# A two-layer matmul with gelu: the opening takes half the rows of a and twice the columns of b, the other rows come later

## Chip, cores and metric

The kernel runs on one core of a Trainium2 chip. The metric is the device time of one execution in microseconds. Times in one set of rounds come from one chip; the sets fell on several chips, so each kernel is compared with the kernel before as it ran in the same rounds.

Terms: PE is the tensor engine (matmuls and transposes), DVE the vector engine (casts and copies), ACT the scalar engine (gelu, casts and copies), SP the queue that issues loads and stores. PSUM is the memory that PE writes. A float32 load is cast to bf16 before PE can use it, so "cast at" tells when a load was usable. A later load is one after the opening; k is the contraction index, cut in eight slices of 128.

## The reference, cut to what matters

```
a: 1024 x 1024, b: 1024 x 2048, c: 2048 x 1024, all float32
h = a @ b
h = 0.5 * h * (1 + tanh(sqrt(2/pi) * (h + 0.044715 * h**3)))
out = h @ c
```

## The kernel before

All matmuls run in bf16 with float32 sums. The first layer makes h transposed, tile by tile: a column tile t of b (128 columns) is the stationary operand, and half of a's rows, transposed, is the moving operand of 512 columns. That gives 16 tiles x 2 halves x 8 contraction slices = 256 matmuls. The second layer has another 256, counted as full width. a has to be transposed by PE first, which takes 64 transposes of 128 x 128.

The opening loads one contraction slice of all of a and of three column tiles of b per step, and fills six PSUM banks (three tiles, two halves):

```python
    for k in range(KT):
        ...                                     # k == 0 in three parts, one of them on the ACT queue
            nc.sync.dma_start(out=st, in_=av[:, :, ts(k, 128)])   # 512-byte runs
            nc.sync.dma_start(out=bt, in_=bv[:, k, 0:W0])         # W0 = 384: 1536-byte runs
    ...
    for _ in range(7):                          # warm-up
        nc.tensor.matmul(wps, warm[:, 0:128], warm, start=True, stop=True)
    ...
    for k in range(KT):
        ...                                     # casts of a and b
        for h in range(2):
            pt = tpool.tile([128, H], BF16, name="pt")
            for j in range(4):
                nc.tensor.transpose(pt[:, ts(j, 128)], ab[:, 4 * h + j, :], ident)
            ...                                 # copy to aT[k][h], DVE or ACT
        if k > 0:
            mm0(k - 1, 1)
        mm0(k, 0)
    mm0(KT - 1, 1)
```

After it come the other 13 column tiles of b, in loads of growing run length through four staging buffers, then c, and each tile is multiplied with both halves of a (`mm1`), followed by gelu on ACT. The second layer and the stores end the kernel.

## Time and profile before

| | before |
|---|---|
| time, median of 4 runs in the rounds with the change | 132.34 us (132.29 to 132.39) |
| span in the profile | 130.6 us |
| first matmul after the opening | 26.86 us |
| first matmul of the second layer | 71.93 us |
| last work of PE | 127.23 us |

From 26.86 us on PE never waits, so all that can be gained lies before, and whatever is added to PE's work later is lost one for one. The prediction below shows the lines.

### The profile page before, as it was taken

The page shows a single profiled execution, that of the slowest core. Times are in us where ns is not written, and L with a number is a line of the kernel's source. Part 1 is how long each engine was busy: PE and PEld are TensorE (multiplying, and loading weights), DVE is VectorE, ACT ScalarE, POOL GpSimd, SP SyncE. Part 2 cuts the span into 40 slices and gives each one's busy share as a digit, 9 for nine tenths or more (in the row PEclk, how much of TensorE's full clock was granted, in tenths as well). Part 3 has the DMA queues.
Part 4 walks back from the last instruction along what each step waited for, and adds up shares of the span by engine and source line. Part 5 has one row for each costly group of instructions (what it writes and reads, how often), then busy time and mean ns, then how long its engine had stood idle before and what let it go on. Part 6 is the DMA issues. An engine that isn't in the chain of part 4 may idle for free.

```text
span 130.6 us, 1457 instructions
## 1 busy us (share of the span) xinstructions
PE 120.7 (92%) x599; PEld 56.1 (43%) x599; DVE 39.0 (30%) x58; ACT 29.0 (22%) x50; POOL 0.7 (1%) x6
## 2 busy tenths in 40 slices
PE   6479998879999999999999999999999999999990
PEld 2144443334444444444444444444444444444580
DVE  0154544243543355345500022222222222211121
ACT  4135453863333333333333100000000000000000
POOL 2000000000000000000000000000000000000000
PEclk9977999999999999999999999999999999999999
DMA  2999999999999999999000022221111222222231
GB/s 40 287 308 310 307 310 309 295 303 359 393 385 398 408 410 405 412 409 360 25 0 0 5 80 80 80 80 72 58 55 64 79 80 80 80 80 80 80 123 40
DMA packets 20390, 25.25 MB, mean 193 GB/s; under 512 B 800, under 2 KB 14368, under 8 KB 20384
## 3 DMA queue, kind: packets, MB, share of 16 engines
q1 hardware_dynamic: 20240, 24.97, 56.7%
q10 hardware_dynamic: 144, 0.20, 1.0%
q8 instruction: 4, 0.07, 0.2%
q14 instruction: 2, 0.02, 0.1%
HBM read 20.97 MB, written 4.19 MB: 193 GB/s over the span
## 4 chain that ended last, share of the span: by engine, by line
PE 77%; DMA 16%; DVE 2%; SPq 1%; ACT 0%; issue 0%; DVEq 0%
PE ps L149 42%; PE ps L126 35%; DMA a_st<-in_a_dram 10%; DMA st<-in_b_dram 6%; SPq L65 1%; DVE ab L84 1%; PE pt L90 1%; DVE b_sb L108 1%; ACT aT L94 0%; SPq L62 0%; SPq L60 0%; DVE ot L141 0%; DVE ab L85 0%; DVEq L84 0%
## 5 line engine op out<-in xcount | busy, mean ns | idle before, releaser
L149 PE MATMUL ps<-c_sb,hT 128*128 128x512 bf16 (+1 forms) x272 | 55.5, 366 | 0.0
L126 PE MATMUL ps<-aT,b_sb 128*128 128x512 bf16 x208 | 45.1, 379 | 1.3 <-DVE b_sb L108 1.3
L149 PEld LDWEIGHTS <-hT 128*128 128x128 bf16 x272 | 26.6, 98 | 28.9
L126 PEld LDWEIGHTS <-b_sb 128*128 128x128 bf16 x208 | 20.3, 98 | 26.1 <-DVE b_sb L108 1.8
L141 DVE COPY ot<-ps 128x512 f32<-128x512 f32 (+1 forms) x17 | 11.2, 660 | 51.5 <-PE ps L149 51.5
L128 ACT ACTIVATE hT<-ps 128x512 bf16<-128x512 f32 x26 | 15.5, 597 | 29.4 <-PE ps L126 29.4
L114 DVE CAST c_sb<-st 128x2048 bf16<-128x2048 f32 x8 | 9.8, 1227 | 10.7 <-DMA st<-in_c_dram 10.7
L79 PE MATMUL ps<-aT,b_sb 128*128 128x512 bf16 x48 | 12.7, 402 | 0.0
L108 DVE CAST b_sb<-st 128x2048 bf16<-128x2048 f32 (+1 forms) x8 | 8.2, 1027 | 12.4 <-DMA st<-in_b_dram 12.4
L90 PE MATMUL pt<-ident,ab 128*128 128x128 bf16 x64 | 6.1, 232 | 4.0 <-DVE ab L84 3.5
L90 PEld LDWEIGHTS <-ab 128*128 128x128 bf16 x64 | 4.0, 102 | 8.9 <-DVE ab L84 7.4
L84 DVE CAST ab<-a_st 128x512 bf16<-128x512 f32 x8 | 3.4, 427 | 10.8 <-DMA a_st<-in_a_dram 10.8
L79 PEld LDWEIGHTS <-b_sb 128*128 128x128 bf16 x48 | 4.6, 103 | 4.4 <-issue 0.8
L86 ACT ACTIVATE b_sb<-b_st 128x384 bf16<-128x384 f32 x8 | 4.2, 523 | 8.2 <-DMA b_st<-in_b_dram 8.2
L94 ACT ACTIVATE aT<-pt 128x512 bf16<-128x512 bf16 x8 | 4.8, 597 | 4.5 <-PE pt L90 4.5
L73 PE MATMUL pt<-warm 128*128 128x512 bf16 x7 | 3.2, 630 | 1.2 <-DVE warm L45 1.2
L92 DVE COPY aT<-pt 128x512 bf16<-128x512 bf16 x8 | 3.4, 423 | 1.9 <-PE pt L90 1.9
L85 DVE CAST ab<-a_st 128x512 bf16<-128x512 f32 x8 | 3.4, 420 | 0.5 <-DMA a_st<-in_a_dram 0.5
L120 ACT ACTIVATE hT<-ps 128x512 bf16<-128x512 f32 x6 | 3.0, 615 | 0.3 <-PE ps L79 0.3
L73 PEld LDWEIGHTS <-warm 128*128 128x128 bf16 x7 | 0.9, 140 | 2.6 <-issue 1.4
L70 ACT ACT_TABLE_LOAD x1 | 1.3, 1283 | 1.2 <-PEq L166 1.2
L45 DVE MEMSET warm<- 128x256 uint32 x1 | 0.3, 272 | 0.9 <-PEq L166 0.9
(7 smaller groups left out, 1.1 us busy)
## 6 DMA issues: line engine op xcount, KB each, us to landing
st<-in_c_dram SPq DMA_DIRECT2D x8, 1024.0 KB, 9.1
st<-in_b_dram SPq DMA_DIRECT2D x5, 1024.0 KB, 9.4
out_dram<-ot SPq DMA_DIRECT2D x15, 256.0 KB, 2.0
a_st<-in_a_dram SPq DMA_DIRECT2D x7, 512.0 KB, 6.2
st<-in_b_dram SPq DMA_DIRECT2D x3, 512.0 KB, 8.6
b_st<-in_b_dram SPq DMA_DIRECT2D x7, 192.0 KB, 6.3
a_st<-in_a_dram SPq DMA_DIRECT2D x2, 256.0 KB, 5.2
out_dram<-ot SPq DMA_DIRECT2D x2, 128.0 KB, 1.9
```

The lines of the kernel that those rows point to most:

```text
L73: nc.tensor.matmul(wps, warm[:, 0:128], warm, start=True, stop=True)
L79: nc.tensor.matmul(ps[t][h], b_sb[:, k, ts(t, 128)], aT[k][h], start=(k == 0), stop=(k == KT - 1))
L84: nc.vector.tensor_copy(ab[:, 0:4, :], a_st[k][:, 0:4, :])
L86: nc.scalar.activation(b_sb[:, k, 0:W0], b_st[k], AF.Copy)
L90: nc.tensor.transpose(pt[:, ts(j, 128)], ab[:, 4 * h + j, :], ident)
L94: nc.scalar.activation(aT[k][h], pt, AF.Copy)
L108: nc.vector.tensor_copy(b_sb[:, kh:kh + kn, ds(t0 * 128, w)], sv)
L114: nc.vector.tensor_copy(c_sb[:, t0:t0 + 2, :], sv)
L126: nc.tensor.matmul(p, b_sb[:, k, ts(t, 128)], aT[k][h], start=(k == 0), stop=(k == KT - 1))
L128: nc.scalar.activation(hT[t][h], p, AF.Gelu_apprx_tanh)
L141: nc.vector.tensor_copy(ot, p)
L149: nc.tensor.matmul(p, hT[t][h][:, ts(j, 128)], c_sb[:, t, ds(q0, w)], start=(t == 0), stop=(t == NT - 1))
```

## The change

Its intent: let PE start the dense part sooner. The opening needs only half the rows of a (2 MB in place of 4), and takes six column tiles of b with them (3 MB in place of 1.5), so the same 48 matmuls stand on fewer bytes, in longer runs. Then come four more column tiles for this half, then the last six. The other rows of a are loaded after all of b, as whole rows (4096-byte runs), and are transposed ("turned") one block of 128 rows after each of the last four groups of the first half. Then the second half runs over all 16 tiles. Three smaller things change with it: slice 0 of b goes over the SP queue like all the rest (before, over ACT's), DVE makes all copies of transposes (before, ACT made half of them), and there are ten warm-up matmuls in place of seven.

```diff
-    N0 = 3
+    N0 = 6
+    N1 = 4
-            nc.sync.dma_start(out=st, in_=av[:, :, ts(k, 128)])
-            nc.sync.dma_start(out=bt, in_=bv[:, k, 0:W0])
+    for k, n in ((0, 1), (1, 1), (2, 2), (4, 2), (6, 2)):
+        load_a0(k, n)              # rows 0 to 511, n slices: runs of n x 512 bytes
+        for i in range(n):
+            load_b0(k + i)         # 768 columns: 3072-byte runs
-    for _ in range(7):
+    for _ in range(10):
...                                # opening: 4 transposes and 6 matmuls a slice
+    for k in range(0, KT, 2):      # second block: 4 tiles, contraction outside
+        load_b(k, 2, W0, W1)
+        ...
+    for n0 in range(W0 + W1, N, W2):        # third block: 6 tiles, W2 = 384
+        for k in range(0, KT, 4):
+            load_b(k, 4, n0, W2)
+    for j in range(4):                      # the other half of a
+        nc.sync.dma_start(out=st, in_=av[:, 4 + j, :])
+    def turn(j):
+        nc.vector.tensor_copy(ab, a1[j])
+        for k in range(KT):
+            nc.tensor.transpose(pt[:, k, :], ab[:, ts(k, 128)], ident)
+        nc.vector.tensor_copy(aT[1][:, :, ts(j, 128)], pt)
+    for t in range(N0 + N1, NT):
+        mm1(t, 0)
+        if t >= NT - 4:
+            turn(t - (NT - 4))
+    for t in range(NT):
+        mm1(t, 1)
```

More of the change, by code (lines that the diff above doesn't have):

```diff
@@ L25 @@
     H = 512
-    N0 = 3
+    N0 = 6
     W0 = N0 * 128
+    N1 = 4
+    W1 = N1 * 128
     av = a.rearrange("(mt p) k -> p mt k", p=128)
@@ L34 @@
     consts = ctx.enter_context(tc.tile_pool(name="consts", bufs=1))
+    keep = ctx.enter_context(tc.tile_pool(name="keep", bufs=1))
     astage = ctx.enter_context(tc.tile_pool(name="astage", bufs=4))
     abf = ctx.enter_context(tc.tile_pool(name="abf", bufs=3))
-    keep = ctx.enter_context(tc.tile_pool(name="keep", bufs=1))
-    b0stage = ctx.enter_context(tc.tile_pool(name="b0stage", bufs=4))
+    b0stage = ctx.enter_context(tc.tile_pool(name="b0stage", bufs=5))
     stage = ctx.enter_context(tc.tile_pool(name="stage", bufs=4))
@@ L47, with load_a0, load_b0 @@
     make_identity(nc, ident)
-    aT = [[keep.tile([128, H], BF16, name=f"aT{k}_{h}") for h in range(2)] for k in range(KT)]
+    aT = [keep.tile([128, KT, H], BF16, name=f"aT{h}") for h in range(2)]
     b_sb = keep.tile([128, KT, N], BF16, name="b_sb")
     c_sb = keep.tile([128, NT, P], BF16, name="c_sb")
-    hT = [[keep.tile([128, H], BF16, name=f"hT{t}_{h}") for h in range(2)] for t in range(NT)]
-    a_st, b_st = [], []
-    for k in range(KT):
-        st = astage.tile([128, MT, 128], F32, name="a_st")
-        bt = b0stage.tile([128, W0], F32, name="b0_st")
-        if k == 0:
-            nc.sync.dma_start(out=st[:, 0:4, :], in_=av[:, 0:4, ts(k, 128)])
-            nc.scalar.dma_start(out=bt, in_=bv[:, k, 0:W0])
-            nc.sync.dma_start(out=st[:, 4:8, :], in_=av[:, 4:8, ts(k, 128)])
-        else:
-            nc.sync.dma_start(out=st, in_=av[:, :, ts(k, 128)])
-            nc.sync.dma_start(out=bt, in_=bv[:, k, 0:W0])
-        a_st.append(st)
-        b_st.append(bt)
+    hT = [keep.tile([128, NT, H], BF16, name=f"hT{h}") for h in range(2)]
+    a_st, b_st = {}, {}
+    def load_a0(k, n):
+        st = astage.tile([128, 4, 256], F32, name="a_st")
+        nc.sync.dma_start(out=st[:, :, 0:n * 128], in_=av[:, 0:4, ds(k * 128, n * 128)])
+        for i in range(n):
+            a_st[k + i] = st[:, :, ts(i, 128)]
+    def load_b0(k):
+        st = b0stage.tile([128, W0], F32, name="b0_st")
+        nc.sync.dma_start(out=st, in_=bv[:, k, 0:W0])
+        b_st[k] = st
+    for k, n in ((0, 1), (1, 1), (2, 2), (4, 2), (6, 2)):
+        load_a0(k, n)
+        for i in range(n):
+            load_b0(k + i)
     g = consts.tile([128, 1], F32, name="g")
@@ L71, with mm0 @@
     wps = tpool.tile([128, H], F32, name="pt")
-    for _ in range(7):
+    for _ in range(10):
         nc.tensor.matmul(wps, warm[:, 0:128], warm, start=True, stop=True)
-    ps = [[ppool.tile([128, H], F32, name="ps") for _ in range(2)] for _ in range(N0)]
-    def mm0(k, h):
+    ps = [ppool.tile([128, H], F32, name="ps") for _ in range(N0)]
+    def mm0(k):
         for t in range(N0):
-            nc.tensor.matmul(ps[t][h], b_sb[:, k, ts(t, 128)], aT[k][h],
+            nc.tensor.matmul(ps[t], b_sb[:, k, ts(t, 128)], aT[0][:, k, :],
@@ L80, in mm0 @@
                              start=(k == 0), stop=(k == KT - 1))
     for k in range(KT):
-        ab = abf.tile([128, MT, 128], BF16, name="ab")
-        nc.vector.tensor_copy(ab[:, 0:4, :], a_st[k][:, 0:4, :])
-        nc.vector.tensor_copy(ab[:, 4:8, :], a_st[k][:, 4:8, :])
-        nc.scalar.activation(b_sb[:, k, 0:W0], b_st[k], AF.Copy)
-        for h in range(2):
-            pt = tpool.tile([128, H], BF16, name="pt")
-            for j in range(4):
-                nc.tensor.transpose(pt[:, ts(j, 128)], ab[:, 4 * h + j, :], ident)
-            if h == 0:
-                nc.vector.tensor_copy(aT[k][h], pt)
-            else:
-                nc.scalar.activation(aT[k][h], pt, AF.Copy)
@@ L95 @@
-        if k > 0:
-            mm0(k - 1, 1)
-        mm0(k, 0)
-    mm0(KT - 1, 1)
-    def load_b(t0, nt):
-        w = nt * 128
-        kn = 2048 // max(w, 256)
-        for kh in range(0, KT, kn):
-            st = stage.tile([128, 2048], F32, name="st")
-            sv = st[:, 0:kn * w].rearrange("p (k n) -> p k n", k=kn)
-            nc.sync.dma_start(out=sv, in_=bv[:, kh:kh + kn, ds(t0 * 128, w)])
-            nc.vector.tensor_copy(b_sb[:, kh:kh + kn, ds(t0 * 128, w)], sv)
+        ab = abf.tile([128, 4, 128], BF16, name="ab")
@@ new lines, with gelu @@
+        nc.vector.tensor_copy(ab, a_st[k])
+        pt = tpool.tile([128, H], BF16, name="pt")
+        for j in range(4):
+            nc.tensor.transpose(pt[:, ts(j, 128)], ab[:, j, :], ident)
+        nc.vector.tensor_copy(aT[0][:, k, :], pt)
+        for i in range(2):
+            nc.scalar.activation(b_sb[:, k, ts(i, W0 // 2)], b_st[k][:, ts(i, W0 // 2)], AF.Copy)
+        if k > 0:
+            mm0(k - 1)
+    mm0(KT - 1)
+    def gelu(t, h, p):
+        nc.scalar.activation(hT[h][:, t, :], p, AF.Gelu_apprx_tanh)
@@ new lines, with load_b @@
+    for t in range(N0):
+        gelu(t, 0, ps[t])
+    def load_b(k0, kn, n0, w):
+        st = stage.tile([128, 2048], F32, name="st")
+        sv = st[:, 0:kn * w].rearrange("p (k n) -> p k n", k=kn)
+        nc.sync.dma_start(out=sv, in_=bv[:, k0:k0 + kn, ds(n0, w)])
+        nc.vector.tensor_copy(b_sb[:, k0:k0 + kn, ds(n0, w)], sv)
+    ps = [(tpool if t < 2 else ppool).tile([128, H], F32, name="pt" if t < 2 else "ps")
+          for t in range(N1)]
+    for k in range(0, KT, 2):
+        load_b(k, 2, W0, W1)
+        for i in range(2):
+            for t in range(N1):
+                nc.tensor.matmul(ps[t], b_sb[:, k + i, ds(W0 + t * 128, 128)], aT[0][:, k + i, :],
+                                 start=(k + i == 0), stop=(k + i == KT - 1))
@@ L110, in load_c, with mm1 @@
+    for t in range(N1):
+        gelu(N0 + t, 0, ps[t])
+    def mm1(t, h):
+        p = ppool.tile([128, H], F32, name="ps")
+        for k in range(KT):
+            nc.tensor.matmul(p, b_sb[:, k, ts(t, 128)], aT[h][:, k, :],
+                             start=(k == 0), stop=(k == KT - 1))
+        gelu(t, h, p)
+    W2 = 384
+    for n0 in range(W0 + W1, N, W2):
+        for k in range(0, KT, 4):
+            load_b(k, 4, n0, W2)
     def load_c(t0):
@@ L114, in load_c @@
         nc.vector.tensor_copy(c_sb[:, t0:t0 + 2, :], sv)
-    load_b(3, 1)
-    load_b(4, 1)
-    for h in range(2):
-        for t in range(N0):
-            nc.scalar.activation(hT[t][h], ps[t][h], AF.Gelu_apprx_tanh)
-    def mm1(t):
-        for h in range(2):
-            p = ppool.tile([128, H], F32, name="ps")
-            for k in range(KT):
-                nc.tensor.matmul(p, b_sb[:, k, ts(t, 128)], aT[k][h],
-                                 start=(k == 0), stop=(k == KT - 1))
-            nc.scalar.activation(hT[t][h], p, AF.Gelu_apprx_tanh)
-    load_b(5, 1)
-    load_b(6, 2)
-    load_b(8, 4)
-    load_b(12, 4)
+    a1 = []
+    for j in range(4):
+        st = astage.tile([128, K], F32, name="a_st")
+        nc.sync.dma_start(out=st, in_=av[:, 4 + j, :])
+        a1.append(st)
+    def turn(j):
+        ab = abf.tile([128, K], BF16, name="ab1")
+        nc.vector.tensor_copy(ab, a1[j])
+        pt = tpool.tile([128, KT, 128], BF16, name="pt")
+        for k in range(KT):
+            nc.tensor.transpose(pt[:, k, :], ab[:, ts(k, 128)], ident)
[4 more added lines that the diff above has]
+            turn(t - (NT - 4))
     for t in range(0, NT, 2):
         load_c(t)
-    for t in range(N0, NT):
-        mm1(t)
+    for t in range(NT):
+        mm1(t, 1)
     def store(mt, q0, w, p):
-        ot = opool.tile([128, w], F32, name="ot", padded_shape=[128, H])
-        nc.vector.tensor_copy(ot, p)
-        nc.sync.dma_start(out=out[ts(mt, 128), ds(q0, w)], in_=ot)
+        ot = opool.tile([128, H], F32, name="ot")
+        nc.vector.tensor_copy(ot[:, 0:w], p)
+        nc.sync.dma_start(out=out[ts(mt, 128), ds(q0, w)], in_=ot[:, 0:w])
     for mt in range(MT):
@@ L148 @@
             for t in range(NT):
-                nc.tensor.matmul(p, hT[t][h][:, ts(j, 128)], c_sb[:, t, ds(q0, w)],
+                nc.tensor.matmul(p, hT[h][:, t, ts(j, 128)], c_sb[:, t, ds(q0, w)],
                                  start=(t == 0), stop=(t == NT - 1))
```

## The prediction

> **What bounds the kernel now.** I read the page's strip of slices first, then the chain that ended last, then the DVE timeline, because the casts there start when a load lands. The strip, from the page of the kernel before (busy tenths in 40 slices of 3.27 us; granted clock in tenths; GB/s of all loads and stores):
> ```profile
> PE   6479998879999999999999999999999999999990
> ...
> PEclk9977999999999999999999999999999999999999
> DMA  2999999999999999999000022221111222222231
> GB/s 40 287 308 310 307 310 309 295 303 359 393 385 398 408 410 405 412 409 360 25 0 0 5 80 80 80 80 72 58 55 64 79 80 80 80 80 80 80 123 40
> ```
> From slice 9 on PE is full. Only the first eight slices have holes, and there the DMA runs at about 309 GB/s, against 393 to 412 later: same engines, other run lengths. The chain (start, us, what):
> ```profile
> 9.12 6.23 DMA a_st<-in_a_dram
> ...
> 18.33 7.76 DMA st<-in_b_dram
> 26.09 0.02 issue
> 26.11 0.70 DVE b_sb L108
> 26.81 0.05 issue
> 26.86 45.07 PE ps L126 x208
> 71.93 55.31 PE ps L149 x272
> 127.23 0.02 issue
> 127.26 0.42 DVE ot L141
> ```
> Up to 26.86 loads set the pace; after that PE never waits. 45.07/208 is 216.7 ns a matmul, and the last one ends at 127.23; the remaining 3.37 us of the 130.6 us span (the last copy, the last store, the close) are not touched. So the change is worth what it moves the end of PE's work, and the timed 132.33 us moves with it. The DVE timeline, whole opening to first c load (start, length):
> ```profile
> 20.10 0.43 DVE L84 CAST ab<-a_st 128x512 bf16<-128x512 f32 x1 [0.98 <-DMA a_st<-in_a_dram]
> ...
> 22.43 0.43 DVE L84 CAST ab<-a_st 128x512 bf16<-128x512 f32 x1 [0.99 <-DMA a_st<-in_a_dram]
> ...
> 26.11 0.69 DVE L108 CAST b_sb<-st 128x1024 bf16<-128x1024 f32 x1 [2.33 <-DMA st<-in_b_dram]
> 27.74 0.69 DVE L108 CAST b_sb<-st 128x1024 bf16<-128x1024 f32 x1 [0.94 <-DMA st<-in_b_dram]
> 29.46 0.69 DVE L108 CAST b_sb<-st 128x1024 bf16<-128x1024 f32 x1 [1.03 <-DMA st<-in_b_dram]
> 32.35 1.23 DVE L108 CAST b_sb<-st 128x2048 bf16<-128x2048 f32 x1 [2.20 <-DMA st<-in_b_dram]
> 35.06 1.23 DVE L108 CAST b_sb<-st 128x2048 bf16<-128x2048 f32 x1 [1.48 <-DMA st<-in_b_dram]
> 37.78 1.23 DVE L108 CAST b_sb<-st 128x2048 bf16<-128x2048 f32 x1 [1.49 <-DMA st<-in_b_dram]
> ```
> One slice of k (512 KB of a in 512-byte runs, 192 KB of b in 1536-byte runs) lands every 2.33 us. PE needs less: eight transposes at about 0.07 and six matmuls at 0.217, 1.86 us.
>
> **What the skill says.** Four places bear on this.
> (1) The Trainium skill, "DMA: Bandwidth & Descriptors", section "Why small descriptors are slow (HBM only)": each packet carries a fixed overhead. The trace agrees. With 16 engines, 512 KB in 512-byte runs is 64 packets an engine in 1.69 us (27.74 less 26.11, and 29.46 less 27.74, averaged): 26.4 ns each. 1 MB in 4096-byte runs (c, casts at 45.76 and 48.31) is 16 packets in 2.56 us: 160 ns. The straight line is 7.3 ns plus 0.0373 ns a byte. It gives 83.7 ns at 2048 bytes; measured 2.70/32 = 84.4.
> (2) Same page, section "Why a DMA increments its semaphore by 16 and not by 1": a load counts as landed only when each of its engines is done, so a slow engine delays the landing though the mean rate holds. The trace suggests it: the first load after the opening was usable 3.17 us after the last opening b (ACT cast at 22.92), where its own bytes need 1.69; the rate stayed near 295 GB/s meanwhile.
> (3) The Trainium skill, "TensorE: Matmul & The Clock Gate", Part 1 (the HAM clock gate): a window of some 3.4 us with too little PE work halves the clock for the next. Here the windows view shows a granted clock of 0.50 from 8.0 to 11.0, with full clock on both sides: about 3.4 us.
> (4) The Trainium skill, "VectorE: DVE Perf Modes", section "Why PSUM operands drop a tier": bf16 out of PSUM goes at most two elements a cycle. The trace has 423 ns for 512 bf16 (L92) against 691 for 512 float32 (L141), which fits.
>
> **The change, part by part.**
> *Opening.* It takes 2 MB of a and 3 MB of b, 5 MB in place of 5.5 MB, and in longer runs. Packets per engine: two a slices alone, 32 of 512 bytes each, 0.845 us; three a pairs, 32 of 1024 bytes (45.5 ns), 1.456; eight b slices, 8 of 3072 bytes (121.9 ns), 0.975. Sum 1.69 + 4.37 + 7.80 = 13.86 us. The same line gives 2.21 for a slice of before, measured 2.33, so I add 5%: 14.55. Before, eight slices were 18.64 and the last b landed at 22.92, an offset of 4.28. After, the last b lands between 18.1 and 18.8; I take **18.5**, 4.4 us sooner.
> *PE in the opening.* Four transposes (0.29) and six matmuls (1.30) a slice, 1.59, against a supply of about 1.75: PE has nearly no slack to catch up. Transposes of slice 1 come before the matmuls of slice 0; a slice 1 lands near 7.2 (two a slices and one b, from data that begin to flow at 3.1, plus about 1.1 of landing), so matmuls start near 8.1. The three more warm-up matmuls bridge only to about 5.2. I expect the half clock from 7.9 to 11.3 again; it costs some 1.7 us, because here PE, not only DMA, is full. End of the opening on PE: 8.1 + 8 x 1.30 + 6 x 0.29 + 1.7 = about 21.9. By DMA it would be 18.5 + two casts of 0.52 (L86) + 1.3 = 20.9. Before, the equivalent point was 26.86: **5 us gained so far**.
> *Second block, 32 matmuls on 512 columns, 6.93 us.* Four loads of 512 KB, 1.35 us each, prefetched into four free buffers; casts 0.69. Hidden, unless the landing delay of (2) comes.
> *Third block, 768 columns.* Four loads of 768 KB in 1536-byte runs, 32 packets of 64.6 ns, 2.07 each. They reuse the four buffers, so the first of them waits for a landing, a cast, an issue and about 2 us until its data flow, against 4.05 us of loads then queued: a gap of 0 to 1 us in the queue.
> *Other half of a.* Four loads, 1.28 us each, only after all of b's 5 MB. The first turn stands after the third matmul group of the third block. Its data land at 18.5 + 5.4 + 8.3 + 1.3 = 33.5 at best, 35.0 with the 1.5 us of (2), up to 36 with the gap. With a 0.69 cast and 0.1 of signals, PE can begin it at 34.3 to 36.8, I take **35.1**. PE's own work would be there at 21.9 + 6.93 + 24 x 0.2167 = 34.0. So PE waits about 1 us, and **DMA sets this point again**. What was moved out of the opening is owed here, since 10.5 MB must have come by then.
> *New work of PE.* The 32 transposes of this half are no longer in the shadow of the opening's loads: 4 x 0.57 = 2.3 us on the path. The last turn's copy out of PSUM (1024 bf16: by (4) twice the streaming part of L92, about 0.69) must end before the second half's first matmul: about 0.95 us of bubble with drain and signals.
> *Sum.* From the first turn: 2.3 + 24 x 0.2167 (5.2) + 0.95 + 128 x 0.2167 (27.7) + 55.3 = 91.5. PE ends at 35.1 + 91.5 = **126.6**, before 127.23. Predicted time 132.33 - 0.6 = **131.7 us**. The c loads, 8 x 2.56 behind a's end near 39, land by 60, and are wanted near 71: hidden.
>
> **Rivals.**
> (A) *No landing delay and no gap; PE warm all along.* Then the opening ends at 20.9 and nothing stalls but the bubble: 20.9 + 208 x 0.2167 + 2.3 + 0.95 + 55.3 = 124.5, or 129.6 us, just over 2% faster. For it: the steady spacing of later loads follows the packet line closely. Against it: all of its luck must come together, and the first turn would need its data by 32.3, before my best 33.5.
> (B) *The loads starve PE in the third block as well.* With both 1.5 us and a gap of 2 us or more, the first turn starts at 37.5 or later and the time is 134 or more. For it: the dip of slice 7 and the rate of 233 GB/s from 27 to 28, where before's own buffers turned over. Against it: the slower stages have long queues, and one buffer gap does not repeat.
> (C) *PE rather than DMA sets the first turn*, because the half clock lasts a second window. That adds 1.7 us on PE, 35.7, which is within the DMA range: 132.3.
>
> **Range and chances.** The path runs through the later of two points, both between 34 and 36.8, so most outcomes lie within 1.5 us of 131.7. I give 130.2 to 133.3. Under 129.7 (faster by over 2%) needs rival A whole: 0.08. Over 135.0 needs a bad B: 0.04. Within 2%: 0.88.
>
> **What would show it right or wrong.** The last opening matmul near 22, not 25.6; the half clock again near 8 to 11; the first b cast of the second block near 20 to 22; PE idle before the first turn, put down to the cast of a or its load, about 1 us; PE idle of about 0.95 before the second half's first matmul, put down to DVE; 32 transposes with full PE around them; c casts with no PE waiting. I am wrong if PE shows no idle from 22 to 36 (rival A), if it stalls by over 2.5 us there (rival B), or if any stage shows a wait on PSUM or on gelu that I have not listed.

## The result, and the profile after

| | before | after |
|---|---|---|
| median of 4 runs | 132.34 us | 131.90 us (131.75 to 132.04) |
| ratio to before | | 0.9967, 95% interval 0.9949 to 0.9984 |
| PE starts the 208 first-layer matmuls that follow the opening's 48 | 26.86 | 21.96 |
| first matmul of the second layer | 71.93 | 71.19 |
| last work of PE | 127.23 | 126.49 |

A ratio is the mean time of one kernel's runs over that of the other's in the same rounds, so it is not quite the ratio of the medians quoted beside it. Executions over 1.5% slower than the fastest of the same kernel are left out of the means. The change is 0.3% faster, the same at 2%. Even this 0.3% hangs on the rounds: the kernel before has two kinds of runs, near 130.7 and near 132 us (see the repeat below), and all four here were of the slower kind. The opening ended 4.90 us sooner, and 0.74 us of it was left when the second layer began.

The strip of slices of the changed kernel, which answers to the first fence of the prediction:

```profile
PE   6857899998799799999999999999999999999990
...
PEclk9999999999999999999999999999999999999999
DMA  4899999999999999970000022222111122222231
GB/s 121 205 358 379 379 391 386 337 375 386 412 409 409 411 404 411 410 288 0 0 0 5 0 81 81 81 81 81 74 58 59 59 80 81 81 81 81 81 121 43
```

After a slow start (slices 0 and 1) the loads of the opening now run at 358 to 391 GB/s, where they ran at about 309. PE still has holes up to slice 4, counted from 0 (the opening), and new ones in slices 9, 10 and 13, after the opening. The clock row has no half-clock window in this run.

PE's timeline of the changed kernel (start, length; what ended the idle time before). L85 and L93 are the opening, L120 the second block, L129 the groups of the third block and of the second half, L155 the turns:

```profile
7.74 1.46 PE L85 MATMUL ps<-aT,b_sb 128*128 128x512 bf16 x6
10.62 0.40 PE L93 MATMUL pt<-ident,ab 128*128 128x128 bf16 x4 [1.42 <-DVE ab L90]
...
19.37 2.75 PE L85 MATMUL ps<-aT,b_sb 128*128 128x512 bf16 x12
21.96 0.59 PE L120 MATMUL pt<-aT,b_sb 128*128 128x512 bf16 x2
...
28.87 1.03 PE L129 MATMUL ps<-aT,b_sb 128*128 128x512 bf16 x4
30.23 4.49 PE L129 MATMUL ps<-aT,b_sb 128*128 128x512 bf16 x20 [0.34 <-DVE b_sb L112]
35.46 0.62 PE L155 MATMUL pt<-ident,ab 128*128 128x128 bf16 x8 [0.74 <-DVE ab L152]
...
43.38 4.92 PE L129 MATMUL ps<-aT,b_sb 128*128 128x512 bf16 x21 [0.79 <-DVE aT L156]
```

Three waits stand between the opening and the second half: for the second half of the third block's first b (0.34), for the first block of a's other rows (0.74), and for the last turn's copy (0.79). The chain that ended last, in order of time, shows what they hang on:

```profile
25.56 9.12 DMA a_st<-in_a_dram
34.68 0.02 issue
34.71 0.70 DVE ab L152
35.41 0.05 issue
35.46 0.62 PE pt L155 x8
...
42.15 0.46 PE pt L155 x8
42.61 0.02 issue
42.64 0.70 DVE aT L156
43.34 0.05 issue
43.38 0.60 PE ps L129 x2
```

The first of the late loads of a is the piece that ends at 34.68. Before the change loads set the pace until 26 us; now they do until nearly 35 us.

The 4.90 us can be followed in steps of PE's issue (a matmul takes 0.2167 us, so waits come out a little longer than the idle times in brackets, which begin only at the modelled end of the last matmul, 0.38 us after its start):

| where | worked out | given back, us |
|---|---|---|
| wait in the third block | 30.23 - (28.87 + 4 x 0.2167) | 0.49 |
| wait before the first turn | 35.46 - (30.23 + 20 x 0.2167) | 0.90 |
| 32 transposes, in four turns | 4 x 0.45 | 1.80 |
| copy of the last turn | 43.38 - (41.99 + 0.45) | 0.94 |
| sum | | 4.13 |

The measured loss is 4.90 - 0.74 = 4.16 us, so this account of the profile is complete to 0.03 us.

### The profile page after: what moved, and what is told of

It is laid out like the page before. It is cut to its first block, busy times and chain, and to the rows that moved or that the text cites. A ratio compares the mean times of both kernels' runs of the same rounds, so it can differ in the third digit from the quotient of the medians.

```text
span 129.8 us, 1447 instructions
## 1 busy us (share of the span) xinstructions
PE 119.4 (92%) x591; PEld 56.4 (43%) x602; DVE 39.5 (30%) x58; ACT 27.2 (21%) x50; POOL 0.7 (1%) x6
## 4 chain that ended last, share of the span: by engine, by line
PE 69%; DMA 21%; SPq 4%; DVE 2%; issue 1%
PE ps L177 42%; PE ps L129 25%; DMA st<-in_b_dram 8%; DMA a_st<-in_a_dram 7%; DMA b_st<-in_b_dram 7%; SPq L67 2%; SPq L61 2%; PE pt L155 2%; DVE ab L152 1%; DVE b_sb L112 1%; DVE aT L156 1%; DVE ot L169 0%; SPq L111 0%
## 5 line engine op out<-in xcount | busy, mean ns | idle before, releaser
L129 PE MATMUL ps<-aT,b_sb 128*128 128x512 bf16 x172 | 38.6, 379 | 1.3 <-DVE aT L156 0.8
L129 PEld LDWEIGHTS <-b_sb 128*128 128x128 bf16 x176 | 17.0, 98 | 21.3 <-DVE aT L156 1.0
L102 ACT ACTIVATE hT<-ps 128x512 bf16<-128x512 f32 x30 | 17.3, 601 | 29.3 <-PE ps L129 28.2
L85 PE MATMUL ps<-aT,b_sb 128*128 128x512 bf16 x47 | 11.4, 379 | 0.1
L96 ACT ACTIVATE b_sb<-b_st 128x384 bf16<-128x384 f32 x16 | 7.5, 515 | 10.2 <-DMA b_st<-in_b_dram 10.0
L112 DVE CAST b_sb<-st 128x1024 bf16<-128x1024 f32 (+1 forms) x8 | 6.6, 827 | 7.8 <-DMA st<-in_b_dram 7.8
L93 PE MATMUL pt<-ident,ab 128*128 128x128 bf16 x32 | 3.4, 232 | 3.4 <-DVE ab L90 3.4
L85 PEld LDWEIGHTS <-b_sb 128*128 128x128 bf16 x48 | 4.4, 98 | 4.0
L79 PE MATMUL pt<-warm 128*128 128x512 bf16 x10 | 4.4, 631 | 1.2 <-DVE warm L47 1.2
L90 DVE CAST ab<-a_st 128x512 bf16<-128x512 f32 x8 | 3.4, 423 | 5.9 <-DMA a_st<-in_a_dram 5.9
L93 PEld LDWEIGHTS <-ab 128*128 128x128 bf16 x32 | 2.3, 104 | 6.4 <-DVE ab L90 5.2
L120 PE MATMUL ps<-aT,b_sb 128*128 128x512 bf16 x16 | 4.8, 379 | 0.1
L120 PEld LDWEIGHTS <-b_sb 128*128 128x128 bf16 x32 | 3.1, 98 | 3.8
L120 PE MATMUL pt<-aT,b_sb 128*128 128x512 bf16 x15 | 4.5, 379 | 0.0
L156 DVE COPY aT<-pt 128x1024 bf16<-128x1024 bf16 x4 | 2.8, 692 | 3.4 <-PE pt L155 3.4
L155 PE MATMUL pt<-ident,ab 128*128 128x128 bf16 x32 | 2.5, 219 | 0.7 <-DVE ab L152 0.7
L155 PEld LDWEIGHTS <-ab 128*128 128x128 bf16 x32 | 2.0, 98 | 1.9 <-DVE ab L152 1.5
```

The source lines that it names most:

```text
L85: nc.tensor.matmul(ps[t], b_sb[:, k, ts(t, 128)], aT[0][:, k, :], start=(k == 0), stop=(k == KT - 1))
L93: nc.tensor.transpose(pt[:, ts(j, 128)], ab[:, j, :], ident)
L96: nc.scalar.activation(b_sb[:, k, ts(i, W0 // 2)], b_st[k][:, ts(i, W0 // 2)], AF.Copy)
L102: nc.scalar.activation(hT[h][:, t, :], p, AF.Gelu_apprx_tanh)
L112: nc.vector.tensor_copy(b_sb[:, k0:k0 + kn, ds(n0, w)], sv)
L120: nc.tensor.matmul(ps[t], b_sb[:, k + i, ds(W0 + t * 128, 128)], aT[0][:, k + i, :], start=(k + i == 0), stop=(k + i == KT - 1))
```

## The experiments

My theory: the path runs over the loads up to the first turn; PE's own opening has slack behind them; after it come the transposes and the bubble of the last copy. The rivals are given with each run.

### Seven warm-up matmuls

```diff
-    for _ in range(10):
+    for _ in range(7):
```

> The changed kernel with 7 warm-up matmuls, as before the change, in place of 10. Theory 1 (the three more warm-ups kept the clock, and the first turn is set by loads): the granted clock falls to about 0.5 for some 3.4 us near 8 to 11, the last opening matmul comes about 1 us later than 21.96, but the first turn still starts near 35.4, because PE has 0.5 + 0.9 us of waits for loads ahead of it; the time stays at 131.9 to 132.3. Rival (PE's opening sets the end): the delay passes through in full, 132.9 or more. Third outcome: the clock stays full, then the warm-ups are not what kept it and the time does not move.

Median 132.31 us (131.6 to 132.8), ratio to before 1.006 (1.0001 to 1.012). The clock fell: the mean granted clock is 0.974 to 0.987 in all six runs. PE's timeline of that kernel:

```profile
8.46 2.76 PE L85 MATMUL ps<-aT,b_sb 128*128 128x512 bf16 x6
...
19.47 2.75 PE L85 MATMUL ps<-aT,b_sb 128*128 128x512 bf16 x12
22.06 0.59 PE L120 MATMUL pt<-aT,b_sb 128*128 128x512 bf16 x2
```

The last line is the start of the second block; in the changed kernel it is at 21.96 us, so the opening ended 0.10 us later. Six matmuls at half clock (the first line) took 2.76 us in place of 1.46, but in the changed kernel PE waits in just that stretch for the first pair of a, which lands near 10.1 us. So the half clock cost the opening a tenth of a microsecond, not 1.7, and not the 1 us expected for this run either. The repeat profile of the changed kernel itself, with ten warm-ups, says the same without any edit:

```profile
8.18 2.66 PE L85 MATMUL ps<-aT,b_sb 128*128 128x512 bf16 x6
...
21.94 0.60 PE L120 MATMUL pt<-aT,b_sb 128*128 128x512 bf16 x2
```

These six matmuls too ran at half the pace, and the opening ended at 21.94 us, where it ended at 21.96 with six at full pace. The clock row of that profile reads 1.00 throughout: its records begin at 10.60 us. So a mean clock of 1.0 does not rule out an early half-clock window; the lengths of the matmuls tell.

With seven warm-ups the first turn came at 36.47, 1.0 later than in the changed kernel, though PE was on time: the fifth later load was cast at 28.12 us instead of 27.14. More on that below. Nor do ten warm-ups keep the clock: among the runs of the changed kernel and its variants with ten, means of 0.987 and of 1.0 both occur. In time, 132.31 lies at the upper edge of what theory 1 allowed; the changed kernel's 131.9 and 131.66 come from other rounds. The profile of seven warm-ups is of the longest run (132.80), and its distance to the changed kernel is that of the late load.

### All opening slices of a alone

```diff
-    for k, n in ((0, 1), (1, 1), (2, 2), (4, 2), (6, 2)):
+    for k, n in [(k, 1) for k in range(KT)]:
```

> The changed kernel with all eight opening slices of a loaded alone in 512-byte runs, not three pairs in 1024-byte runs. By the packet line, six slices cost 6 x 0.845 = 5.07 us instead of 4.37, so every later landing moves by 0.7 us. If loads set the first turn, the time rises by 0.7 us to about 132.6. If run length does not matter for the end (loads hidden behind PE), it stays at 131.9.

Median 132.75 us (132.48 to 133.55), ratio to before 1.0124 (1.0067 to 1.0181), against 131.9 and 131.66 for the changed kernel in two other sets. The first later load was cast at 21.47 us in place of 20.38 and the first turn began at 36.66 in place of 35.46. Longer runs are worth about 1 us of the end, a little more than the 0.7 of the packet line. Of the 1.2 us at the first turn, 1.1 were already there at the first later load, so they come from the opening's loads. It supports that loads set this stretch.

### The last turn earlier

```diff
-    for t in range(N0 + N1, NT):
-        mm1(t, 0)
-        if t >= NT - 4:
-            turn(t - (NT - 4))
+    ... mm1(12, 0), turn(0), mm1(13, 0), turn(1), mm1(14, 0), turn(2), turn(3), mm1(15, 0)
+    # the cast of turn 3 is issued before the copy of turn 2
```

> The changed kernel with the last turn before the last matmul group of the first half, so that its copy out of PSUM lies beside that group. Theory: the 0.94 us between the last turn and the second half's first matmul is a plain bubble on the path: 0.9 us less, 131.0. Rival: the wait only moves, to the cast or to the third turn: 131.7 or more.

Median 130.93 us (130.58 to 131.51), ratio to before 0.9975, as the kernel before had its own good runs in these rounds (see below). Against the changed kernel's 131.9 it is 1.0 us. PE goes from the last two turns through the last group into the second half with no wait. The bubble was real.

### The first late load of a before the last loads of b

```diff
     for n0 in range(W0 + W1, N, W2):
         ...
+        if n0 == W0 + W1:
+            load_a1(0)
+            cast(0)
```

> The changed kernel with the first whole-row load of a, and its cast, ahead of the last two loads of b. Theory: the 0.90 us that PE waits before the first turn goes, the last b loads land 1.3 us later and are usable at about 35.7, just before PE wants them at 35.9: 0.9 us less, 131.0. Rival: the queue is what is late as a whole, the wait moves to the b loads after the first turn, and the time stays within 0.3 us of 131.9.

Median 130.86 us (130.61 to 131.93), ratio to before 0.9981. The first turn began at 34.26 us, straight after the third block's first three groups, with no wait; the bubble of 0.79 was still there. Also 1.0 us, where 0.9 was expected. In this profile no later load was late, so the third block's wait of 0.49 was gone too; that part need not be the edit's.

### The changed kernel and the kernel before once more

> The changed kernel once more, beside the chip and rounds of the experiments, because the kernel before showed two times there, about 130.7 and 132.3. If the two times come from the chip or from a landing delay that either kernel can have, the changed kernel spreads too, between about 131.0 and 132.8, and the ratio lies within 1% of 1. If the changed kernel has no such delay, it stays at 131.9 within 0.2.

> The kernel before, unchanged, for a second profile. If the profiled run is one near 130.7, the theory of a landing delay says that the first load after the opening then lands about 1.7 us after the last opening load, not 3.2, with the clock making no difference; the rival (the clock's half window) says that the landings are the same and PE differs. If it is one near 132.3 it shows nothing new.

The changed kernel: 131.66 us (131.45 to 131.83), ratio to before 1.001 (0.9953 to 1.0066). The kernel before in the same rounds: 132.02 us median, but 130.57 to 132.24. In the four sets of the experiments it ran near 130.5 to 130.8 us in 11 of 42 runs and near 132 in the rest. Runs with a recorded half-clock window (mean 0.987) lie in both kinds, so having such a window is not what parts them. The changed kernel, in ten runs, had no such fast kind. The extra profile of the kernel before (132.35 us) fell on the slower kind again and shows nothing new; no profile caught the faster one. The 3.17 us that the first load after the opening took in the slower kind, for 1.69 us of bytes, would be just the difference, but this is not shown. Beside the faster kind, the changed kernel is 1 us slower, not faster.

### Five staging buffers

```diff
-    stage = ctx.enter_context(tc.tile_pool(name="stage", bufs=4))
+    stage = ctx.enter_context(tc.tile_pool(name="stage", bufs=5))
```

> The changed kernel with five staging buffers for the later loads in place of four, so that the fifth load need not wait for the first one's cast. Theory of the queue gap: the dip in the rate near 25 to 26 us goes, the fifth load lands about 0.5 us sooner, PE's wait in the third block (0.5) goes and the first turn starts 0.5 us sooner: 131.4. Rival (the delay is an engine that is late, not the queue): the landing times stay, 131.9.

Median 131.97 us (131.06 to 132.82), no better than the changed kernel's 131.66. DVE's timeline of its profile, which is of the longest of the six runs (casts of the third, fourth and fifth later load):

```profile
23.12 0.69 DVE L112 CAST b_sb<-st 128x1024 bf16<-128x1024 f32 x1 [0.65 <-DMA st<-in_b_dram]
26.04 0.69 DVE L112 CAST b_sb<-st 128x1024 bf16<-128x1024 f32 x1 [2.23 <-DMA st<-in_b_dram]
28.11 0.96 DVE L112 CAST b_sb<-st 128x1536 bf16<-128x1536 f32 x1 [1.38 <-DMA st<-in_b_dram]
```

The loads before the fourth landed 1.35 us apart; the fourth came after 2.92, 1.6 us late, with its buffer free from the start. So this late landing is not the turnover of the buffers. In the changed kernel it is the fifth load that comes late (cast at 27.14 after 24.42, 2.72 where its bytes need 2.07). There the rate also falls, to 280 GB/s from 25 to 26 us, which is about 0.3 of the 0.65 us; with five buffers that dip is gone (372). So the buffers may account for a part of the changed kernel's small delay, not for the delay of 1.6. Over the profiles of the changed kernel and its variants the delay at the fourth to sixth later load is between 0 and 1.6 us, and it stays with all loads after it.

In each of these profiles the view of the DMA queues shows one packet of the queue that it names instruction, in a window of half a microsecond that starts at 20.0 to 23.5 us. For the changed kernel, from 23.0 to 23.5 us (queue: packets, MB, share of the 16 engines' time):

```profile
q1 hardware_dynamic: 99, 0.16, 89.6%
q8 instruction: 1, 0.02, 13.8%
```

13.8% of 16 engines for 0.5 us is 1.1 us of one engine: so long was this packet under way. A load has landed when the last engine is done with its part (point 2 of the prediction), so a load could be late by that much while the mean rate barely moves: with five buffers it was 384, 366 and 372 GB/s from 23 to 26 us, after 387.

### The instruction packet moved

```diff
-    for _ in range(10):
-        nc.tensor.matmul(wps, warm[:, 0:128], warm, start=True, stop=True)
+    for _ in range(40):
+        nc.tensor.matmul(wps[:, 0:128], warm[:, 0:128], warm[:, 0:128], start=True, stop=True)
```

> The changed kernel with 40 warm-up matmuls of 128 columns in place of 10 of 512: about as long, but 60 more instructions of PE ahead of everything. In every profile so far one packet of the instruction queue takes one of the 16 DMA engines for about 1.1 us, at 22.5 to 23.5 us, and the loads then due land 0 to 1.6 us late. If that packet is what makes them late, it now comes some 6 us sooner (about 16 to 17 us), and the late landing, where there is one, is that of an opening load or of the first later load; the fifth load then follows the fourth by about 2.1 us. Rival (the turnover of the staging buffers, or the place in the queue, makes the delay): the packet moves and the delay stays at the fourth or fifth later load.

The packet came at 20.0 us, three sooner, not six. The fourth and fifth later loads were then cast at 25.20 and 27.29, 2.09 apart: no delay at that place. But none showed elsewhere either, and another variant (the first late load of a early) had the packet at 22.5 us and no delay. Three runs took 131.38, 131.98 and 132.47 us, ratio to before 0.9989 (0.9962 to 1.0017); a fourth, of 133.43, was slow. The experiment does not settle the cause. That the packet makes loads late fits its length and its place, but it is not shown. The opening was late from its very start in this run (second slice of a cast at 8.46 us, 7.02 in the changed kernel), for which I have no cause.

### Both single edits

```diff
+    # first late load of a early, and the last turn early, as above
```

> The changed kernel with the first whole row of a early and the last turn early, the two single edits that took 1.0 us each. If they are separate places on the path, they add: 1.8 to 2.0 us under the changed kernel of the same rounds, about 130. If both only shift the same wait, about 131.

Median 130.37 us (129.99 to 131.46), ratio to before 0.9927 (0.987 to 0.9984), and 1.3 us under the changed kernel of the same rounds: less than the 1.8 to 2.0 expected. In its profile, of a run of 130.86 us, the fourth later load was late by 1.5 us, and PE paid for it in the third block:

```profile
28.86 1.04 PE L129 MATMUL ps<-aT,b_sb 128*128 128x512 bf16 x4
30.96 4.49 PE L129 MATMUL ps<-aT,b_sb 128*128 128x512 bf16 x20 [1.06 <-DVE b_sb L112]
```

### Contraction outside in the third block

This and the next kernel have both single edits too; the fence shows what is added to them.

```diff
+    for k0 in (0, 4):
+        for t in range(T1, T2):           # tiles 10 to 12: slices k0 to k0 + 3
+            part(ps, T1, t, k0)
+    turn(0)
+    ...                                   # tiles 13 to 15 in the same way, turns between the half groups
```

> Both single edits, and the third block with contraction outside: three column tiles take the first four slices, then the other four, so that PE wants the sixth load 1.7 us later than in group order. Theory (PE wants data in the third block as early as they can land, so each late landing passes to the end): PE no longer waits in the third block even with a late landing, about 129.5 in nearly every run, 2.3 us under the changed kernel and less spread than the kernel with both edits (130.0 to 131.5). Rival (first turn or second half bounds it by now): no better than 130.4.

Median 130.22 us (130.03 to 130.56, four runs), ratio to before 0.9862 (0.9849 to 0.9875). The third block's wait is gone although a load was late in the profile (fifth cast at 27.24 after 23.96), and the spread is smaller, but 129.5 was missed, because the wait reappeared at the next turn:

```profile
37.05 0.62 PE L167 MATMUL pt<-ident,ab 128*128 128x128 bf16 x8 [1.27 <-DVE ab L144]
```

> The last one, with the matmuls of the first two opening slices straight after their transposes, in the wait for the first pair of a. Theory: PE has up to 1.3 us of waits near 6 and 9 us, the opening then ends about 0.7 us sooner at the loads' own pace (near 21), and with the third block's slack the end moves by 0.3 to 0.7: 129.0. Rival: the loads bound the third block, no change against 129.5.

That variant, which only reorders the first two opening slices, gave 130.22 us (129.96 to 131.27), ratio 0.9882. Its opening did not end sooner (second block from 22.16 us): PE had work in the early wait, and waited for later loads instead. So here too loads set the opening, not PE's order of work.

### The turns later

The order of PE's calls in the kernel with contraction outside, and the new one (written short; the casts on DVE move with the turns):

```diff
-    part(13, k 0..3)  part(14, k 0..3)  turn(1)  part(15, k 0..3)  part(13, k 4..7)  turn(2)  turn(3)  part(14, k 4..7)  part(15, k 4..7)
+    part(13, k 0..3)  part(14, k 0..3)  part(15, k 0..3)  part(13, k 4..7)  turn(1)  part(14, k 4..7)  turn(2)  turn(3)  part(15, k 4..7)
```

> The kernel with contraction outside, with turns 1 to 3 put one to two half groups later. In its profile PE waited 1.27 us before turn 1, whose cast ended at 37.0, while half groups that need no new data stood behind that turn. Theory: PE works on them first, reaches turn 1 at about 37.0 to 37.4 and no longer waits; the second half starts at about 41.3 in place of 41.86, 129.6 us or a little less. Rival: the last turns then come too late and the wait moves to them or to the second half's first matmul; 130.2, no change.

Median 129.91 us (129.26 to 130.06) beside 132.14 for the kernel before, ratio 0.983 (0.9774 to 0.9885): it beats both kernels, though the interval reaches to either side of 2%, and 0.3 us above the expected 129.6. Beside the faster kind of the kernel before it is 0.6% less. PE's waits in the whole execution (us in total, times, longest) show what is left after the opening, which is nothing:

```profile
PE pt L93 <- DVE ab L90: 2.2, 3, 1.5
PE pt L79 <- DVE warm L47: 1.2, 1, 1.2
```

The second half starts at 41.44 us (predicted 41.3), 1.94 us sooner than in the changed kernel. What remains is the opening itself and the 1.8 us of transposes.

## Why the prediction was right, point by point

The time was predicted at 131.7 us and is 131.9; the end of PE's work at 126.6 and is 126.49. Two things of this closeness are luck. The sum starts from 132.33 us, which is the slower kind of the kernel before, and all four runs beside the change happened to be of that kind. And in the opening four errors cancelled, as the second point shows.

- **Loads set the first turn.** Right. It was put at 35.1 us within 34.3 to 36.8, and came at 35.46 in the changed kernel, 36.66 when the runs were made shorter, and 34.26 when its load was moved up. The load landed at 34.68, 1.2 us after the prediction's best case of 33.5: 0.5 of it at the first later load, 0.65 at the fifth.
- **The opening.** Its end on PE, 21.9, came out (21.96) by luck. The step "It costs some 1.7 us, because here PE, not only DMA, is full" failed: in the profiled run six matmuls from 7.74 us took 1.46 us, at full clock, and where they took 2.66 or 2.76 the opening ended at 21.94 or 22.06. PE was not full. What stands in place of the 1.7 us is waits for loads, 2.48 us in steps of issue: 1.58 before the third slice, 0.49 and 0.41 before the fifth and the seventh. The start was 0.36 sooner than the predicted 8.1, and six times four transposes took 1.35 in place of 1.74. So 7.74 + 10.40 + 1.35 + 2.48 makes 21.97, where the prediction had 8.1 + 10.40 + 1.74 + 1.7. Between 3.5 and 5.5 us the loads ran at only 92 to 185 GB/s, which I had not foreseen and for which I have no cause.
- **Wait before the first turn, about 1 us.** Right: 0.74 idle, 0.90 in steps of issue. The further 0.49 in the third block belonged to rival B; it was there in a small form.
- **New work on the path.** Four turns at 0.57 were mis-sized; they take 0.45 each, 1.8 us in all. The bubble, 0.95, measured 0.94, and moving the last turn took 1.0 us off the time.
- **The landing delay of 0 to 1.5 us.** Right as a range (up to 1.6), and five buffers showed a delay of 1.6 that the buffers do not make. Its cause stays open between the instruction packet and something not seen.
- **Two readings of the strip.** "Only the first eight slices have holes" leaves out slice 8 (busy tenths 7), the wait before 26.86 us; and the later rates are 385 to 412 GB/s, not 393 to 412. Neither enters the sum.
- **Rival A (faster by over 2%).** It needed all waits gone. Only after four edits on top of the change did the time come to 129.9.

The change is small in effect because it moved work out of a stretch that loads set, into one that PE sets (the transposes), and left the next need for bytes just as urgent.

## What to carry to other kernels

An opening that needs fewer bytes only helps if the bytes that it puts off are not wanted soon after: add up the bytes due by each later point, and compare with PE's work up to there. Work moved out of the shadow of loads into a dense PE stretch costs its full time. Where the arrival of loads scatters, order PE's work so that what needs no new data stands first; that and two earlier placements took about 2 us off here (131.66 to 131.9 in other rounds, against 129.91), where the change itself gave 0.4 us in its own rounds and nothing clear in the repeat.

## What the Trainium skill lacked or had wrong

- "Runtime: NRT & Kernel Launch", section "Instruction fetch mechanics", says that instructions come in 16 KiB blocks over a DMA queue of the sequencer's own, and that crossing into a new block is mostly hidden. It does not say what a block costs other transfers: here such a packet (0.02 MB) was under way for 0.9 to 1.1 us, 21.5 to 27.5 us apart in the profile of the kernel with contraction outside (23.0, 44.5, 69.5 and 97.0 us), the first two in the midst of loads. That it delays them is not shown.
- "DMA: Bandwidth & Descriptors", Specifications, gives 512 bytes as the least transfer for line rate. Here runs of 512 bytes took 26.4 ns a packet and engine (about 310 GB/s), and runs of 4096 bytes 160 ns (about 410).
- The same page, section "Where 436 GB/s comes from", says without a condition that loads from HBM are bound near 358 GB/s per core; the page's own measured rates tie that figure to two busy cores on one memory. The one busy core here held 404 to 412 GB/s for seven slices of the changed kernel's strip, some 22 us.
- "TensorE: Matmul & The Clock Gate", Part 4, gives about 275 ns for a 128 x 128 bf16 transpose within one kernel. Here eight in a row took 0.45 us of PE's issue, 56 ns each, and one lasted 219 ns from start to end.
- No page tells that a kernel's time can fall into two kinds 1.5 us apart in the same rounds without a difference in recorded mean clock (the kernel before: 11 of 42 runs near 130.7, the rest near 132).
